# A hybrid decoder layer on one core: weight low parts on VectorE, table loads in the emission clock, TensorE ordered by the scheduler

## The chip, the cores and the metric

The kernel runs on one core of a Trainium2 chip. The metric is device time in microseconds, as the median of several executions; lower is better. One further execution was taken by the hardware profiler, and all rows below are of that one. The engines are TensorE (PE; its weight loads are listed as PEld), VectorE (DVE), ScalarE (ACT), GpSimd (POOL) and SyncE (SP), which issues DMAs.

## The reference

One layer over 512 prompt tokens and 32 sample tokens (8 sequences of 4), width 1024, all in float32:

```python
h = rmsnorm(x);  u = h @ w_in        # [HGRN2 q,f,i,g | RWKV-7 r,k,v, lora | gates]
o_a, s_a = hgrn2(u_a, s_a)           # 4 heads, 128x128 state, chunks of 64
o_b, s_b = rwkv7(u_b, s_b)           # 8 heads, 64x64 state, step by step:
#   S = S*w - (S@kk) (kk*a)^T + v k^T ;  y = S@r
x = x + (sigmoid(u_ga) * (o_a @ w_a_out) + sigmoid(u_gb) * (o_b @ w_b_out)) @ w_out
x = x + relu(rmsnorm(x) @ w_up)**2 @ w_down
y = rmsnorm(x)
```

The outputs are y, the new states of both branches and the last normalised row, each for prompt and samples.

## The kernel before

**Products.** All activations lie with channels on the partitions and the 544 tokens in the free dimension, in two halves of 272. Each float32 weight tile `st` (128x1024) is split by `split` into a high part `whi` (a copy on ACT to the matmul type fp32r) and a low part `wlo = st - whi`; a product is three passes, hi·hi, lo·hi and hi·lo. `w_in` is worked off in 46 column units of 128 columns; a unit is two `in_unit_ps` halves of 24 matmuls, 92 halves in all. The weight of a unit is loaded and split a few units ahead, in `ahead()`: there `wlo` is made on VectorE for the first units, and on GpSimd once more than `NDVE` = 11 units have been loaded.

**Lanes.** Between the matmuls of these halves the recurrences are worked off, in three lanes of generators: LX does the RWKV-7 heads in two groups of four (g0 from k0, k1, r0, r1, v0, v1; g1 from k2 to v3), LZ the low-rank parts (`lora_ps`) first, LY the four HGRN2 heads (`hg_head_*`), then the sample states (`rw_state`, `rw_sample`, `hg_sample`). The RWKV-7 steps of a group are, in order: `rw_batch_pa` for each of its head pairs (p0, p1 or p2, p3), the inverse of a triangular matrix on VectorE with DMAs through `zb_d` and `xz_d`, `rw_solve`, `rw_affine`, `rw_chain` and `rw_out`. The last writes `ob_d`, which the B branch reads back as `ob`.

**What sets the order.** While the kernel is built, a `Clock` keeps a planned time per engine. `Timed.cost` gives each instruction a planned duration. `gemm_h` calls `tick()` every 4 or 12 matmuls, and `tick` advances each lane whose planned readiness has come. So a lane's step is emitted after that many matmuls of the halves; the same clock chooses the next unit of the plan among `NEED` and `FILL`. From there the tile framework's scheduler orders the instructions of each engine by its own estimate of readiness. TensorE is taken out of that: the region of `manual_schedule(engines={PE})`, from the start of the lanes up to `drain(LY)` behind the B branch, leaves PE in the order of emission.

**Stages.** Norm and transposes (to 27 us), `w_in` with the lanes (to 541 us), the rest of g1 and of the samples, the B branch (16 groups `half_unit_ps` of 12 matmuls), the A branch (16 more), `w_out` (`pd`, from 655 us), `w_up`, `w_down` and the last norm. PSUM: `pse` is a single double bank, which `rw_batch_pa`, `lora_ps` and other steps of LX and LZ take in turn.

All instructions are issued by the helper `Timed.call`, so nearly all rows have its line (L160), and are told apart by the tile names.

Of the kernel before, what the change touches and what calls it, by code (L numbers as in the profile page):

```python
# [8 lines left out]
F32 = mybir.dt.float32  # L9
# [3 lines left out]
AF = mybir.ActivationFunctionType  # L13
ALU = mybir.AluOpType
# [30 lines left out]
PQ, LQ, ZQ, TQ = 0, 0, 1, 0  # L45
POOL_LO = 1
QUANT, FINE = 12, 4
NDVE = 11
NEED = "l0 k0 k1 r0 v0 r1 v1 l1 f0 q0 i0 g0 f1 q1 i1 g1 f2 q2 i2 g2 k2 k3 r2 r3 v2 v3 f3 q3 i3 g3"
FILL = "G8 G10 G2 G1 G3 G7 G13 G4 G11 G15 G9 G12 G5 G6 G14 G0"  # L50
X_WORK = "rw0 rw1"
# [4 lines left out]
class Clock:  # L56


    def __init__(self):
        self.ready, self.used, self.by, self.tags, self.busy = {}, {}, {}, {}, {}  # L60
        self.pe, self.gemm, self.lane, self.late = 0.0, True, None, []
# [4 lines left out]
    def place(self, eng, t, cost):  # L66
        b = self.busy.setdefault(eng, [])
        k = len(b)
        while k and b[k - 1][1] > t:
            k -= 1  # L70
        while k < len(b) and b[k][0] < t + cost:
            t = max(t, b[k][1])
            k += 1
        b.insert(k, (t, t + cost))
        while b and b[0][1] < self.pe - 60:
            b.pop(0)
        return t + cost
# [14 lines left out]
    def note(self, eng, cost, outs, ins, lane):  # L92
        for t in outs:
            self.first(t)
        r = 0.0
        for t, own in [(t, False) for t in ins] + [(t, True) for t in outs]:
            if self.by.get(t.name) != eng or (eng == "DMA" and not own):
                r = max(r, self.ready.get(t.name, 0.0))
            elif eng not in ("PE", "DMA"):
                r = max(r, self.ready[t.name] - 0.12)  # L100
            if own and not (eng in ("PE", "DMA") and self.by.get(t.name) == eng):
                r = max(r, self.used.get(t.name, 0.0))
        if eng == "PE":
            if r > self.pe + 0.2:
                self.late.append((self.pe, r - self.pe, outs[0].name))
            self.pe = end = max(self.pe, r) + cost
            end += 0.15
        elif eng == "DMA":
            end = r + cost
        else:  # L110
            end = self.place(eng, r, cost) + 0.12
        for t in ins:
            self.used[t.name] = max(self.used.get(t.name, 0.0), end)
        for t in outs:
            self.ready[t.name] = end
            self.by[t.name] = eng
            self.used[t.name] = max(self.used.get(t.name, 0.0), end)
        if lane is not None:
            lane.end = max(lane.end, end)


class Timed:


    def __init__(self, eng, name, clock):
        self.eng, self.name, self.clock = eng, name, clock

    def cost(self, fn, out, ops, kw):
        n = 1
        for d in out.shape[1:]:  # L130
            n *= d
        big = max([n] + [int(o.free_size()) for o in ops if hasattr(o, "tensor")])
        if self.name == "PE":
            gemm = len(ops) > 1 and ops[1].dtype == F32R
            switch = 0.12 if gemm != self.clock.gemm else 0.0
            self.clock.gemm = gemm
            if gemm:
                return n / 2400 + 0.013 + switch
            if fn == "transpose":
                return 0.11 * max(n, 32) / 128 + switch  # L140
            return max(n, 32) * (0.00085 if ops[0].shape[-1] >= 128 or n >= 128 else 0.0006) + switch
        if fn == "dma_start":
            return 2.3
        if self.name == "V":
            if fn == "reciprocal":
                return 0.1 + 0.0064 * n
            if fn == "tensor_tensor_scan":
                return 0.1 + 0.0022 * n
            return 0.15 + 0.00106 * big
        if self.name == "A":  # L150
            return 0.17 + 0.0009 * big
        if fn == "tensor_tensor":
            return 0.2 + 0.0025 * big
        return 0.3 + 0.0012 * big
# [25 lines left out]
def hybrid_step(ctx: ExitStack, tc: tile.TileContext, i, o):  # L180
    nc = tc.nc
    clock = Clock()
    V, A, P, T = (Timed(e, n, clock) for e, n in ((nc.vector, "V"), (nc.scalar, "A"), (nc.gpsimd, "P"), (nc.tensor, "PE")))
# [5 lines left out]
    def nm(s):  # L189
        uid[0] += 1  # L190
        return f"{s}{uid[0]}"
# [17 lines left out]
    def S(n, dt=F32, name="s"):  # L209
        return xp_.tile([128, 552], dt, tag="x", name=nm(name))[:, 0:n]  # L210
# [43 lines left out]
    def act(out, in_, func=AF.Copy, **kw):  # L254
        A.activation(out=out, in_=in_, func=func, **kw)

    def tt(out, a, b, op, eng=None):
        (eng or V).tensor_tensor(out=out, in0=a, in1=b, op=op)
# [27 lines left out]
    class W:  # L286
        pass

    def split(st, eng=None):
        w = W()  # L290
        w.hi = pipe.tile([128, 1024], F32R, tag="whi", name=nm("whi"))
        w.lo = pipe.tile([128, 1024], F32R, tag="wlo", name=nm("wlo"), bufs=3)
        act(w.hi, st)
        tt(w.lo, st, w.hi.bitcast(F32), ALU.subtract, eng)
        return w

    def load8(src, c):

        st = pipe.tile([128, 1024], F32, tag="stage", name=nm("st"), bufs=NST)
        SY.dma_start(out=st.rearrange("p (k c) -> p k c", k=8),  # L300
                          in_=src[:, c:c + 128].rearrange("(k p) c -> p k c", p=128))
        return st
# [78 lines left out]
    for u in STARTUP.split():  # L381
        if u == "w":
            pre = split(pre)
        elif u[0] == "s":
            stats(TORD[int(u[1])])
        else:
            {"t": transposed, "n": normed}[u[0]](TORD[int(u[1])], int(u[2]))
# [114 lines left out]
    def load4(src, c):  # L502

        st = pipe.tile([128, 1024], F32, tag="stage", name=nm("st"), bufs=NST)
        SY.dma_start(out=st.rearrange("p (k c) -> p k c", k=4),
                          in_=src[:, c:c + 256].rearrange("(k p) c -> p k c", p=128))
        return st
# [27 lines left out]
    def column(tok):  # L535
        n = int(tok[1:])
        if tok[0] in "lrkv":
            return B0 + 128 * ({"r": 0, "k": 4, "v": 8, "l": 12}[tok[0]] + n)
        return G0 + 128 * n if tok[0] == "G" else A0 + 512 * "qfig".index(tok[0]) + 128 * n

    need, fill, done, held, plan = NEED.split(), FILL.split(), set(), [0], []
    loaded, weights = {}, {column("l0"): pre}
# [13 lines left out]
    def ahead(c):  # L556

        for n, tok in enumerate(plan[0:3]):
            if tok not in loaded:
                loaded[tok] = load8(i["w_in"][0], column(tok))  # L560
        for tok in plan[0:2]:
            if tok in loaded and column(tok) not in weights:
                weights[column(tok)] = split(loaded[tok], P if len(loaded) > NDVE else V)
        return weights.pop(c)

    def in_unit(c, cuts=(0, HALF, TOK)):
        w = ahead(c)
        wh = [w.hi[:, 128 * k:128 * k + 128] for k in range(8)]
        wl = [w.lo[:, 128 * k:128 * k + 128] for k in range(8)]
        return gemm_h(wh, wl, [h_hi[:, k] for k in range(8)], [h_lo[:, k] for k in range(8)], cuts, "in_unit_ps")  # L570
# [26 lines left out]
    for kind in range(2):  # L597
# [3 lines left out]
        w = S(512, F32R, "lwd")  # L601
# [949 lines left out]
    def drain(*ls):  # L1551
        while any(L.work for L in ls):
            L = min((L for L in lanes if L.work and L.ready is not None), key=lambda L: L.ready)
            clock.pe = max(clock.pe, L.ready)
            if not advance(L):
                L.ready = min(M_.ready for M_ in lanes if M_.work and M_ is not L) + 0.01

    region = tc.manual_schedule(engines={mybir.EngineType.PE})
    region.__enter__()
    clock.start()  # L1560
    LZ.work.append(low_rank())
    for L, names in ((LX, X_WORK), (LY, Y_WORK)):
# [6 lines left out]
    while plan:  # L1569
        tok = plan.pop(0)  # L1570
# [55 lines left out]

    ob = branch(ob_d)
    wb = [split(load4(i["w_b_out"][0], 0))]
    for jp in range(4):
        if jp < 3:  # L1630
            wb.append(split(load4(i["w_b_out"][0], 256 * jp + 256)))
        w = wb[jp]
# [7 lines left out]
                r = slice(e * HALF, (e + 1) * HALF)  # L1640
                stt(mb[j][:, r], gt[:, r], 1.0, ps[e], ALU.add, ALU.mult)
    drain(LY)
    region.__exit__(None, None, None)
    pystack.close()
    psm = ctx.enter_context(tc.tile_pool(name="psm", bufs=2, space=bass.MemoryType.PSUM))

# [6 lines left out]
    for jp in range(4):  # L1653
        w = split(load4(i["w_a_out"][0], 256 * jp))
# [169 lines left out]
    for j in range(8):  # L1824
        st = load8(i["w_down"][0, 3072:4096], 128 * j)
        if j < 8 - NKEEP:
            w = []
# [7 lines left out]
        else:  # L1835
            w = split(st)
# [45 lines left out]
```

## Time and profile before

| | before |
| --- | --- |
| median of 3 runs (lowest to highest) | 1102.83 us (1100.08 to 1108.12) |
| profiled execution, device time | 1101.6 us |
| its span in the trace | 1099.9 us |
| PE busy over the span | 957.2 us (87%) |
| DVE, ACT, POOL busy | 577.3, 404.9, 198.5 us |
| share of the chain that ended last | PE 62%, DVE 15%, DMA 7%, ACT 7%, POOL 4% |

The profiled execution is 1.2 us below the median, and 1.7 us of it lie outside its span. Stages below are given in us from the span's start.

### The profile page before, as it was taken

The numbers are of one execution on the slowest core, as the hardware profiler recorded it, in microseconds if no ns is written. First come the engines' busy times: TensorE is split into PE (matmuls) and PEld (weight loads), VectorE is DVE, ScalarE is ACT, GpSimd is POOL, SyncE is SP. The second block draws the span as 40 slices with busy tenths as digits, with TensorE's granted clock in tenths as the row PEclk, the third lists the DMA queues.
The fourth block names the chain that finished last, engine by engine and source line by source line (L and its number), as shares of the span: only waits on it lengthen the run. The fifth ranks groups of instructions, "written<-read, shape, count | busy, mean of one in ns | idle before, by whom it ended". The sixth has DMA issues, their size and how long they took to land.

```text
span 1099.9 us, 21956 instructions
## 1 busy us (share of the span) xinstructions
PE 957.2 (87%) x9220; PEld 923.6 (84%) x9220; DVE 577.3 (52%) x1135; ACT 404.9 (37%) x761; POOL 198.5 (18%) x335
## 2 busy tenths in 40 slices
PE   5887778798987879779949599999999999999996
PEld 4787767787887878769738599999999999999996
DVE  6464639445766585713566585544432234444533
ACT  7451524546444433433231234334311123332332
POOL 4267443222254442221010000000000000000000
PEclk9798788899998889989968799999999999999998
DMA  8421323221133233341265445332333323233411
GB/s 241 135 85 53 101 69 74 74 60 42 60 100 101 78 93 69 92 121 43 79 185 183 156 127 157 88 97 78 96 87 87 95 78 97 79 104 90 133 39 44
DMA packets 191093, 106.40 MB, mean 97 GB/s; under 512 B 38946, under 2 KB 179048, under 8 KB 190995
## 3 DMA queue, kind: packets, MB, share of 16 engines
q1 hardware_dynamic: 165424, 95.16, 29.6%
q10 hardware_dynamic: 25570, 9.85, 3.5%
q8 instruction: 72, 1.18, 0.4%
q14 instruction: 27, 0.21, 0.1%
HBM read 85.08 MB, written 18.39 MB: 94 GB/s over the span
## 4 chain that ended last, share of the span: by engine, by line
PE 62%; DVE 15%; DMA 7%; ACT 7%; POOL 4%; issue 4%; SPq 1%; ACTq 1%; POOLq 0%; DVEq 0%
PE pd L160 21%; PE full_unit_ps L160 14%; PE in_unit_ps L160 14%; PE half_unit_ps L160 3%; DVE tmp L160 2%; DMA st<-in_w_down_dram 2%; ACT whi L160 1%; POOL lmk L394 1%; DVE wlo L160 1%; ACT L160 1%; DVE X L160 1%; DVE rs L160 1%; DVE bn L160 1%; PE lora_ps L160 1%; SPq L160 1%
## 5 line engine op out<-in xcount | busy, mean ns | idle before, releaser
L160 ACT ACTIVATE whi<-st 128x1024 fp32r<-128x1024 f32 x120 | 126.8, 1056 | 267.9 <-PE pd L160 117.7
L160 DVE TENSOR_TENSOR wlo<-st,whi 128x1024 fp32r<-128x1024 f32 x85 | 104.1, 1225 | 65.9 <-ACT whi L160 65.8
L160 PE MATMUL in_unit_ps<-h_hi,wlo 128*128 128x272 f32 (+3 forms) x736 | 122.2, 302 | 0.0
L160 PE MATMUL in_unit_ps<-h_hi,whi 128*128 128x272 f32 (+3 forms) x736 | 117.7, 304 | 3.5 <-ACT h_hi L160 3.3
L160 PE MATMUL in_unit_ps<-h_lo,whi 128*128 128x272 f32 (+3 forms) x736 | 111.6, 295 | 0.0
L160 PE MATMUL full_unit_ps<-hd,whi 128*128 128x272 f32 (+2 forms) x832 | 109.8, 288 | 0.0
L160 PEld LDWEIGHTS in_unit_ps<-h_hi,whi 128*128 128x128 f32 x736 | 104.8, 200 | 5.4 <-ACT h_hi L160 3.8
L160 PEld LDWEIGHTS in_unit_ps<-h_hi,wlo 128*128 128x128 f32 x736 | 105.3, 197 | 2.0 <-issue 0.3
L160 PEld LDWEIGHTS full_unit_ps<-hd,whi 128*128 128x128 f32 x832 | 106.2, 188 | 0.0
L160 POOL TENSOR_TENSOR wlo<-st,whi 128x1024 fp32r<-128x1024 f32 x35 | 85.8, 2451 | 98.6 <-ACT whi L160 97.4
L160 PEld LDWEIGHTS in_unit_ps<-h_lo,whi 128*128 128x128 f32 x736 | 102.3, 195 | 0.1
L160 POOL TENSOR_SCALAR ys<-ys,ssf 32x512 f32<-32x512 f32 x1 | 1.1, 1087 | 532.8 <-DVE ssf L160 532.8
L160 DVE SCALAR_TENSOR_TENSOR r<-pd,rsb 128x272 f32<-128x272 f32 x64 | 25.2, 436 | 90.5 <-PE pd L160 89.1
L160 PE MATMUL pd<-xgh,wlo 128*128 128x272 f32 x512 | 70.1, 288 | 0.0
L160 PE MATMUL pd<-xgh,whi 128*128 128x272 f32 x512 | 69.8, 288 | 0.0
L160 PE MATMUL pd<-xgl,whi 128*128 128x272 f32 x512 | 69.6, 287 | 0.0
L160 PEld LDWEIGHTS pd<-xgh,wlo 128*128 128x128 f32 x512 | 66.4, 188 | 0.0
L160 PEld LDWEIGHTS pd<-xgh,whi 128*128 128x128 f32 x512 | 66.3, 188 | 0.0
L160 PEld LDWEIGHTS pd<-xgl,whi 128*128 128x128 f32 x512 | 66.2, 188 | 0.0
L160 DVE TENSOR_TENSOR x<-x,full_unit_ps 128x272 f32<-128x272 f32 (+2 forms) x48 | 19.5, 435 | 71.6 <-PE full_unit_ps L160 71.6
L160 PE MATMUL full_unit_ps<-hd,wlo 128*128 128x272 f32 (+2 forms) x416 | 56.5, 288 | 0.0
L160 PEld LDWEIGHTS full_unit_ps<-hd,wlo 128*128 128x128 f32 x416 | 53.8, 188 | 0.0
(414 smaller groups left out, 1558.9 us busy)
## 6 DMA issues: line engine op xcount, KB each, us to landing
st<-in_w_in_dram SPq DMA_DIRECT2D x46, 512.0 KB
st<-in_w_up_dram SPq DMA_DIRECT2D x32, 512.0 KB
st<-in_w_down_dram SPq DMA_DIRECT2D x32, 512.0 KB
gt_d<-gt SPq DMA_DIRECT2D x16, 272.0 KB
st<-in_w_out_dram SPq DMA_DIRECT2D x8, 512.0 KB
gtb<-gt_d SPq DMA_DIRECT2D x8, 272.0 KB
gta<-gt_d SPq DMA_DIRECT2D x8, 272.0 KB
x<-xt_d SPq DMA_DIRECT2D x8, 272.0 KB
```

The source lines that it names most:

```text
L160: r = real(*a, **kw)
L394: return tc.keep_in_program_order(getattr(nc.gpsimd, name)(*a, **kw))
```

## The change

Three edits. `split` no longer takes an engine, so all low parts are made on VectorE; 35 of them were made on GpSimd. `Timed.cost` counts 1.3 us where an activation needs another function table than the last one, and 0.2 us for an accumulated output; this adds no instruction, but shifts the planned times, and with them the place of the lane steps among the matmuls and the choice of the next unit. And the manual region is gone, so the scheduler orders PE too.

```diff
-NDVE = 11
@@ class Timed
-        self.eng, self.name, self.clock = eng, name, clock
+        self.eng, self.name, self.clock, self.table = eng, name, clock, 0
@@ def cost
         if self.name == "A":
-            return 0.17 + 0.0009 * big
+            sets = {AF.Tanh: 1, AF.Exp: 1, AF.Sigmoid: 2, AF.Ln: 3, AF.Sqrt: 4}
+            new = sets.get(kw.get("func"), self.table)
+            load, self.table = 1.3 if new != self.table else 0.0, new
+            return 0.17 + 0.0009 * big + load + (0.2 if "accum_out" in kw else 0.0)
@@ def split
-        tt(w.lo, st, w.hi.bitcast(F32), ALU.subtract, eng)
+        tt(w.lo, st, w.hi.bitcast(F32), ALU.subtract)
@@ def ahead
-                weights[column(tok)] = split(loaded[tok], P if len(loaded) > NDVE else V)
+                weights[column(tok)] = split(loaded[tok])
@@ the lanes
-    region = tc.manual_schedule(engines={mybir.EngineType.PE})
-    region.__enter__()
     clock.start()
...
     drain(LY)
-    region.__exit__(None, None, None)
```

The order of the units in the plan is the same for the first 21; from there gates are drawn forward. k2, the first unit of g1, is the 25th before and the 28th after; v3, the last of g1, the 31st and the 35th. Seven units are left behind g3, the last one that a head needs, where nine were.

How PE's order moves is seen at two places. The first is about the eighteenth half, where the `lora_ps` steps of the gate stand. Before, on PE (a row is a run of matmuls, out<-moving,stationary, with its shape and count):

```order
L160 MATMUL in_unit_ps_1250<-h_lo,whi_980 128x272 x8
L160 MATMUL lora_ps_1276<-lx_391,lwh_375 128x272 x2
L160 MATMUL lora_ps_1276<-lx_391,lwl_376 128x272 x2
L160 MATMUL lora_ps_1276<-lx_392,lwh_375 128x272 x2
L160 MATMUL rw_batch_pa_1285<-kr_1009,eb_934 128x128 x8
L160 MATMUL lora_ps_1301<-lx_391,lwh_375 128x272 x2
```

And after, on PE at the same place:

```order
L162 MATMUL in_unit_ps_1248<-h_lo,whi_978 128x272 x8
L162 MATMUL in_unit_ps_1333<-h_hi,whi_1118 128x272 x8
L162 MATMUL in_unit_ps_1333<-h_hi,wlo_1119 128x272 x8
L162 MATMUL in_unit_ps_1333<-h_lo,whi_1118 128x272 x5
L162 MATMUL lora_ps_1274<-lx_391,lwh_375 128x272 x2
L162 MATMUL lora_ps_1274<-lx_391,lwl_376 128x272 x2
L162 MATMUL lora_ps_1274<-lx_392,lwh_375 128x272 x2
L162 MATMUL in_unit_ps_1333<-h_lo,whi_1118 128x272 x3
L162 MATMUL in_unit_ps_1387<-h_hi,whi_1118 128x272 x7
L162 MATMUL rw_batch_pa_1283<-kr_1007,eb_932 128x128 x8
```

The step stands 21 matmuls further back, and matmuls of the halves stand between it and `rw_batch_pa`. The second place is the solve of g1. Before, on PE:

```order
L160 MATMUL in_unit_ps_5555<-h_lo,whi_5300 128x272 x8
L160 MATMUL rw_solve_py_5604<-XT_5573,zb_4550 32x32 x16
L160 MATMUL rw_solve_py_5604<-XT_5573,zb_4790 32x32 x16
L160 MATMUL in_unit_ps_5672<-h_hi,whi_5413 128x272 x8
L160 MATMUL in_unit_ps_5672<-h_hi,wlo_5414 128x272 x4
L160 MATMUL rw_sample_ps_5685<-rs_5640 64x64 x8
L160 MATMUL rw_sample_pt_5695<-ident,bd_5653 128x128 x4
L160 MATMUL rw_solve_px_5702<-TT_5577,YT_5574 32x32 x16
```

And after, on PE, where `in_unit_ps_5767` is the 92nd and last half:

```order
L162 MATMUL in_unit_ps_5767<-h_lo,whi_5540 128x272 x6
L162 MATMUL rw_state_ps_5736<-ident,sn_5731 128x128 x4
L162 MATMUL in_unit_ps_5767<-h_lo,whi_5540 128x272 x2
L162 MATMUL rw_solve_py_5816<-XT_5785,zb_4637 32x32 x16
L162 MATMUL rw_solve_py_5816<-XT_5785,zb_4995 32x32 x16
L162 MATMUL rw_solve_px_5867<-TT_5789,YT_5786 32x32 x16
L162 MATMUL rw_solve_px_5867<-TT_5794,YT_5786 32x32 x16
L162 MATMUL rw_affine_pw_5944<-KA_5123,TT_5789 64x128 x6
```

Before, the solve of g1 stands behind the 84th half, and eight halves are spread over it and the steps behind it; after, all 92 halves are ahead of it. In the same way the last `rw_batch_pa` of g1 (pair p3) stands at half 73 before and 79 after. Most steps of `hg_sample`, which stand among the B branch before, are ahead of it after.

## Rows read from the trace of the kernel before

**Rows 1.** Windows: busy time of each engine (x instructions), granted PE clock, DMA.

```profile
27.00:655.00 628.00, 508.01 (x5680) 478.37 (x5680) 377.22 (x779) 245.94 (x475) 186.09 (x314) 0.89 0.32 93
655.00:1100.00 445.00, 434.65 (x3467) 433.21 (x3467) 182.22 (x292) 139.25 (x240) 1.09 (x1) 0.99 0.32 92
```

**Rows 2.** Windows, finer stretches of the first; columns PE, PEld, DVE, ACT, POOL.

```profile
27.00:419.00 392.00, 318.44 (x3414) 304.57 (x3415) 238.82 (x450) 170.81 (x317) 159.68 (x279) 0.90 0.28 79
419.00:488.00 69.00, 53.74 (x699) 51.42 (x700) 38.50 (x86) 25.86 (x66) 16.19 (x16) 0.93 0.41 100
...
541.00:566.00 25.00, 14.61 (x235) 10.28 (x232) 16.61 (x58) 8.76 (x21) 2.75 (x9) 0.71 0.51 129
...
575.00:623.00 48.00, 34.01 (x243) 31.36 (x243) 29.98 (x64) 7.48 (x12) 0.00 (x0) 0.78 0.51 161
```

**Rows 3.** Waits of PE, 27 to 655 us: total, times, longest.

```profile
PE hg_head_pt L160 <- DVE kh L160: 16.3, 4, 7.7
PE hg_head_pt L160 <- DVE hy L160: 16.1, 3, 8.2
PE lora_ps L160 <- DVE CB L160: 14.6, 2, 12.9
PE half_unit_ps L160 <- ACT oh L160: 11.3, 5, 6.4
PE head_sums_ps L160 <- POOL sxl L160: 6.9, 2, 6.2
```

**Rows 4.** Timeline of PE, 95 to 118 us: start, duration, what, idle before.

```profile
100.13 1.17 PE L160 MATMUL in_unit_ps<-h_hi,wlo 128*128 128x272 f32 x8
101.13 1.16 PE L160 MATMUL in_unit_ps<-h_lo,whi 128*128 128x272 f32 x8
115.24 0.79 PE L160 MATMUL lora_ps<-lx,lwh 128*128 128x272 f32 x2 [12.95 <-DVE CB L160]
```

**Rows 5.** Timeline of POOL, 80 to 118 us.

```profile
107.69 1.69 POOL L394 TENSOR_SCALAR_AFFINE_SELECT lmk<-lmk 32x32 f32<-32x32 f32 x6
109.46 0.40 POOL L160 TENSOR_TENSOR d<-U 128x24 f32<-128x24 f32 x2
```

**Rows 6.** Timeline of DVE, 95 to 118 us.

```profile
109.89 0.79 DVE L160 SCALAR_TENSOR_TENSOR xm<-d,prm,U 128x544 f32<-128x544 f32 x1 [13.72 <-POOL d L160]
```

**Rows 7.** Timeline of PE, pieces between 415 and 660 us.

```profile
417.69 1.16 PE L160 MATMUL rw_batch_pa<-kr,eb 64*128 64x128 f32 x16
...
487.85 1.20 PE L160 MATMUL rw_solve_py<-XT,zb 32*32 32x32 f32 x64
...
560.93 0.37 PE L160 MATMUL rw_out_pt<-ident,yo 64*64 64x64 f32 x2
...
574.68 1.14 PE L160 MATMUL half_unit_ps<-oh,whi 128*128 128x272 f32 x2 [3.64 <-ACT oh L160]
...
654.97 0.51 PE L160 MATMUL pd<-mh,whi 128*128 128x272 f32 x2 [0.30 <-ACT mh L160]
```

**Rows 8.** The page's groups: busy us, mean ns of one, idle before.

```profile
L160 DVE TENSOR_TENSOR wlo<-st,whi 128x1024 fp32r<-128x1024 f32 x85 | 104.1, 1225 | 65.9 <-ACT whi L160 65.8
...
L160 POOL TENSOR_TENSOR wlo<-st,whi 128x1024 fp32r<-128x1024 f32 x35 | 85.8, 2451 | 98.6 <-ACT whi L160 97.4
```

**Rows 9.** Timeline of DVE, 326 to 345 us.

```profile
328.21 2.84 DVE L160 SCALAR_TENSOR_TENSOR xm<-d,prm,U 128x544 f32<-128x544 f32 x1 [2.87 <-POOL d L160]
```

**Rows 10.** Timeline of POOL, 326 to 345 us.

```profile
328.13 2.34 POOL L160 TENSOR_TENSOR wlo<-st,whi 128x1024 fp32r<-128x1024 f32 x1
```

**Rows 11.** Timeline of ACT, 344 to 347 us.

```profile
344.75 1.28 ACT L160 ACT_TABLE_LOAD   x1
346.05 1.18 ACT L160 ACTIVATE nrm<-head_sums_ps 128x512 f32<-128x512 f32 x3
```

**Rows 12.** Timeline of DVE, 415 to 500 us.

```profile
419.90 0.42 DVE L160 TENSOR_TENSOR CB<-rw_batch_pa,msk 128x256 f32<-128x256 f32 x1
...
462.04 1.53 DVE L160 STREAM_TRANSPOSE XT<-D 32x256 f32<-32x256 f32 x4 [4.15 <-DMA D<-xz_d]
```

More of the change, by code (lines that the diff above doesn't have):

```diff
@@ L287, in hybrid_step, with split @@
         pass
-    def split(st, eng=None):
+    def split(st):
         w = W()
```

## The prediction

> **What bounds the kernel now.** I read the windows first. Behind 655 us PE is busy for 434.7 of 445 us at a granted clock of 0.99; nothing is to be had there, and the change doesn't touch that part. From 27 to 655 us PE is busy for 508.0 of 628 us at 0.89, so some 120 us are idle; DVE is busy for 377.2, ACT for 245.9, POOL for 186.1 [rows 1]. No engine is full in this stretch: PE waits for the chains of the recurrences. The finer windows say where. 27 to 419 us holds 73.6 us of idle PE at a clock of 0.90, 419 to 488 another 15.3, 541 to 566 another 10.4 with the clock at 0.71, 575 to 623 another 14.0 with 0.78 [rows 2]. The waits name the ends: HGRN2 steps that wait for DVE (16.3 and 16.1 us), `lora_ps` for DVE's `CB` (14.6, of it 12.9 at once), `head_sums` for POOL (6.9), the branches for `oh` (11.3) [rows 3]. At the longest the reader sees what kind of wait it is: `in_unit_ps` matmuls run until 102 us, then PE stands 12.95 us before a `lora_ps` [rows 4], although the next halves of the GEMM depend on nothing in that chain. POOL was making masks until 109.4 us and only then a small `d`, for which DVE had waited 13.72 us [rows 5, 6]; behind it DVE came to the `CB` that frees the PSUM bank. So these are waits of program order: the step was emitted by a planned time that came too early, and the GEMM behind it was blocked.
>
> **PE ordered by the scheduler.** The `lora_ps` step now stands 21 matmuls further back, and the GEMM runs ahead of it; most steps of the lanes move back by one to six halves in the same way. PE still works in the order written, and that order is a guess on readiness: a step put too early stalls as before. The trace has no run of the new order, so the return lies between nothing and the 73.6 us idle before 419 us [rows 2]. The first two kinds of waits, for `kh` and `hy`, are at the end of long DVE chains that a scheduler sees; the wait behind POOL's masks is one of small instructions whose number, not size, matters. I take 33 us, a bit under half, since the longest wait is of the second kind.
>
> Now the sum, by events on PE. Before, the last `rw_batch_pa` of g1 starts at 417.69 us [rows 7]. In the new order it stands behind 79 halves, not 73. Eight matmuls take 1.00 us from start to start [rows 4], so a half is 3.0 and six are 18 us. With 33 us of idle gone: 417.7 + 18 − 33 = 403.
>
> From there to the solve of g1 it took 70.2 us before [rows 7], with 53.7 busy of 69 [rows 2] and 11 halves in it. Now 13 halves stand there: 6 us more, 59.7 busy; of the 15.3 idle I keep half: 67 us, so 470. The inverse hides in it: from `CB` at 419.90 to the end of the transposes at 463.57 is 43.7 us [rows 12], and 24 us passed before between that end and the solve. That is slack of program order which the new order fills with GEMM.
>
> From the solve to `rw_out` it took 73.1 us [rows 7], with eight halves, 24 us, in it. Now all 92 halves are ahead, so the bounds are 49 us, if every half had lain on the path, and 73, if the chain of DVE, ACT and PE steps sets the time by itself. Steps of `hg_sample` move into this stretch from the B branch, and DVE was busy there for 16.6 of 25 us between 541 and 566 us [rows 2], so I take 60: 530.
>
> From `rw_out` to the first `half_unit_ps` are 13.8 us of DMA out, DMA in and split [rows 7]; unchanged: 544. From there to `w_out` it took 80.3 us [rows 7]. The 32 groups of 12 matmuls at 0.125 us are 48 us; the rest is idle or at the lower clock, 14.0 us of it waits in 575 to 623 [rows 2]. With much of `hg_sample` out of the way the bounds are 48 and 80; I take 68, nearer to the old value because A's operands come last there and PE waited 6.4 us for them [rows 3]: 612. What follows took 1101.6 − 655.0 = 446.6 us [rows 7], unchanged. The sum is 1058.6 against the profiled 1101.6, and with the 1.2 us by which the median stands above it, **1060 us**.
>
> **Low parts on VectorE.** 35 `wlo` leave POOL, 85.8 us, and cost DVE 35 × 1.225 = 42.9 us [rows 8]. What comes back is that DVE is no longer held up by them: one `xm` took 2.84 us while a POOL `wlo` of 2.34 us began 0.08 us ahead of it, where the same operation took 0.79 at another place [rows 6, 9, 10]. So between nothing and 35 × 2.05 = 72 us of DVE time return. In both cases DVE stays under two thirds busy [rows 1], and the weight of a unit is due a few units, some 6 us each, ahead. POOL, busy for 186 of 628 us, is freed. I price it at nothing for PE; the ends are −5 us (a `head_sums` that waits for `sxl` behind a `wlo`, 6.9 us in all [rows 3]) and +5 (a DVE step of a chain behind four 1.2 us subtractions), and they lie within the choices above.
>
> The Trainium skill ("VectorE: DVE Perf Modes", on the second SBUF read interface shared with GpSimd) bears that out for `xm`, which has two SBUF inputs. It would make the return the larger one, and the sum a few us lower.
>
> **Table loads in the clock.** Nothing is added to ACT by itself. A load takes 1.28 us and the next activation starts 1.30 us behind its start [rows 11], so the planned 1.3 is the measured one. Its effect is the later place of the steps and the plan in which g1's units come three to four units later; both are counted above, as the 18 us. If the scheduler had ordered the steps well anyway, this part is a loss of that size.
>
> The Trainium skill ("ScalarE: Activation LUTs", What ACT_TABLE_LOAD costs) puts a switch at 1.28 us and 1.38 of drain, 2.66 in all. The trace disagrees: the activation follows at once [rows 11]. By the page the planned time would be 1.36 us too short per load, steps would stand too early, and more of the 33 us would stay as waits.
>
> **Rivals.** First, slower. The GEMM is the only filler that PE has, and the new order spends all 92 halves before the solve. If the waits ahead of it stay (none of the 73.6 us goes), the last `rw_batch_pa` comes at 436, the solve 75 us later at 511, the chain, naked now and with `hg_sample` on DVE in front of it, takes the old 73: 584, B at 598. With the clock low for its first part as between 541 and 566 us (0.71 [rows 2]) B and A take 80 to 85, and the end is 1125 to 1130. It decides at about 420 us: if `rw_batch_pa` of p3 isn't earlier than that, the halves that went ahead of it are a loss. For it speaks that the new positions are later throughout; against it, that 24 us of known slack go in any case.
>
> The Trainium skill ("TensorE: Matmul & The Clock Gate", HAM oscillation) warns that idle gaps between bursts of matmuls drop the clock to its lower level, which speaks against a chain without filler; the 0.71 and 0.78 of [rows 2] agree with it.
>
> Second, no change. The lanes, not PE, set the stage: the chains of DVE and ACT have their own length, waits only move from one step to the next, and the solve comes when it did, at about 488. Then only the halves behind it shorten the rest: 488 + 66 + 14 + 78 + 447 + 1 = 1094 to 1103. For it speaks that DVE is busy for 60% and its steps depend on each other; against it that PE's waits before 419 us are few and long, and at those the GEMM is ready.
>
> Third, better than forecast: nine tenths of the idle time before 419 us go (66 us), the chain takes 49 and the branches 60: `rw_batch_pa` at 370, solve 430, `rw_out` 479, B 493, `w_out` 553, the end 1001 us. It needs a scheduler that guesses every chain right.
>
> **How the numbers follow.** A measurement of this kernel tells about 1% from no change. Forecast, with its own 1016 to 1091: 0.68; third rival, 0.06; no change, 0.13; slower, 0.13. Faster by over 1% is 0.74, within 1% 0.13, slower 0.13. The range of 1016 to 1106 leaves out most of the slower and of the third case, under 2 in 10.
>
> **What would show it.** The 12.95 us before `lora_ps` and the 6 us before `head_sums` gone or moved to another step; idle PE before the last `rw_batch_pa` of 40 us, not 74; that step at about 403; the solve at 470 behind the last half; a stretch of about 75 us from the solve to B with PE half idle and the clock near 0.7; `w_out` at about 612 and the same 447 us behind it. `xm` at 0.8 us everywhere. The forecast is wrong if waits before 419 us stay above 65 us in new places, or if solve to `w_out` takes over 165 us.

## The result

The changed kernel takes 1054.76 us (1051.74 to 1056.61, 4 runs) against 1102.98 (1100.08 to 1108.12): a ratio of 0.9555 with a 95% interval of 0.9512 to 0.9599. The forecast was 1060. The profiled execution took 1051.7 us with a span of 1050.0.

First the windows of the changed kernel, cut at its own events (the last `rw_batch_pa` of g1, its solve, its `rw_out`, the B branch, the A branch, `w_out`); the columns are those of [rows 1].

```profile
27.00:388.00 361.00, 326.68 (x3544) 313.43 (x3543) 240.94 (x478) 177.38 (x327) 105.08 (x252) 0.95 0.32 92
388.00:451.00 63.00, 58.51 (x739) 57.08 (x738) 41.40 (x91) 25.71 (x63) 4.71 (x10) 0.95 0.44 114
451.00:516.00 65.00, 49.36 (x799) 38.96 (x799) 31.66 (x95) 18.82 (x44) 3.04 (x8) 0.79 0.15 35
516.00:537.50 21.50, 10.61 (x133) 7.45 (x131) 14.39 (x44) 6.19 (x16) 2.34 (x9) 0.52 0.64 182
537.50:575.00 37.50, 34.13 (x245) 30.05 (x243) 27.25 (x59) 8.28 (x13) 0.00 (x0) 0.86 0.65 211
575.00:604.00 29.00, 28.69 (x218) 28.69 (x219) 24.52 (x50) 10.70 (x15) 0.00 (x0) 0.94 0.43 139
604.00:1050.00 446.00, 436.37 (x3481) 434.92 (x3480) 183.34 (x294) 139.90 (x241) 1.09 (x1) 0.99 0.32 92
```

Up to the last `rw_batch_pa` 34.3 us of PE are idle where 73.6 were [rows 2], and the clock is granted at 0.95, not 0.90. Of the idle time behind it most lies between 451 and 537.5 us, where 26.5 of 86.5 us are idle and the clock falls to 0.79 and then 0.52, little above the lower of its two levels (1.2 of 2.4 GHz, which is 0.50). Behind 604 us nothing has changed [rows 1].

The events, in the timeline of PE (they answer to [rows 7]):

```profile
387.99 1.16 PE L162 MATMUL rw_batch_pa<-kr,eb 64*128 64x128 f32 x16
...
451.21 0.98 PE L162 MATMUL rw_solve_py<-XT,zb 32*32 32x32 f32 x50
...
515.81 1.18 PE L162 MATMUL rw_out_pt<-ident,yo 64*64 64x64 f32 x32 [2.37 <-DVE yo L162]
...
528.05 1.97 PE L162 MATMUL rw_out_pt<-ident,yo 64*64 64x64 f32 x32 [0.96 <-DVE yo L162]
...
537.45 0.89 PE L162 MATMUL half_unit_ps<-oh,whi 128*128 128x272 f32 x3
...
600.08 1.66 PE L162 MATMUL pd<-mh,whi 128*128 128x272 f32 x12
```

The last `rw_batch_pa` comes 29.7 us earlier than before, although six halves more stand ahead of it; the solve 36.6, `rw_out` 45.1, B 37.2 earlier.

PE's waits in the changed kernel, 27 to 610 us, against [rows 3]:

```profile
PE head_sums_ps L162 <- POOL sxl L162: 20.1, 4, 13.4
...
PE half_unit_ps L162 <- ACT oh L162: 2.8, 3, 1.7
...
PE hg_head_pt L162 <- DVE kh L162: 2.0, 1, 2.0
PE lora_ps L162 <- DVE CB L162: 1.9, 1, 1.9
...
PE hg_head_pt L162 <- DVE hy L162: 1.1, 1, 1.1
```

32.4 us of waits for `kh` and `hy` have become 3.1; 14.6 for `CB` have become 1.9. One wait has grown by much: `head_sums` for GpSimd's `sxl`, 6.9 to 20.1. It is the old wait behind the masks at another step, as PE and POOL show at 101 us:

```profile
101.86 0.82 PE L162 MATMUL head_sums_ps<-sxl,bones 128*128 128x272 f32 x2 [13.41 <-POOL sxl L162]
```

```profile
99.36 0.57 POOL L396 TENSOR_SCALAR_AFFINE_SELECT lmk<-lmk 32x32 f32<-32x32 f32 x2
...
100.48 1.33 POOL L162 TENSOR_TENSOR sxl<-rk,sxh 128x544 fp32r<-128x544 f32 x1
```

### The profile page after: what moved, and what is told of

It is laid out like the page before. It is cut to its first block, busy times and chain, and to the rows that moved or that the text cites. A ratio compares the mean times of both kernels' runs of the same rounds, so it can differ in the third digit from the quotient of the medians.

```text
span 1050.0 us, 21959 instructions
## 1 busy us (share of the span) xinstructions
PE 959.4 (91%) x9220; PEld 923.6 (88%) x9220; DVE 580.4 (55%) x1170; ACT 406.1 (39%) x763; POOL 127.7 (12%) x300
## 4 chain that ended last, share of the span: by engine, by line
PE 65%; DVE 10%; DMA 3%; ACT 3%; issue 2%; POOL 1%; ACTq 1%; SPq 0%; DVEq 0%; POOLq 0%
PE pd L162 23%; PE full_unit_ps L162 18%; PE in_unit_ps L162 11%; PE half_unit_ps L162 4%; DVE tmp L162 1%; DVE rs L162 1%; PE rw_affine_pw L162 1%; PE rw_affine_pq L162 1%; DVE wlo L162 1%; PE rw_chain_pc L162 1%; DVE E L162 1%; DVE X L162 1%; DVE bn L162 1%; PE hg_sample_po L162 1%; DVE gs L162 1%
## 5 line engine op out<-in xcount | busy, mean ns | idle before, releaser
L162 DVE TENSOR_TENSOR wlo<-st,whi 128x1024 fp32r<-128x1024 f32 x120 | 147.1, 1225 | 82.3 <-ACT whi L162 82.0
L162 PE MATMUL in_unit_ps<-h_hi,wlo 128*128 128x272 f32 (+3 forms) x736 | 118.5, 297 | 0.0
L162 PEld LDWEIGHTS in_unit_ps<-h_hi,wlo 128*128 128x128 f32 x736 | 102.8, 193 | 1.3 <-issue 0.3
L162 ACT ACTIVATE gt<-in_unit_ps 128x272 f32<-128x272 f32 x32 | 12.6, 394 | 47.5 <-PE in_unit_ps L162 35.7
```

The source lines that it names most:

```text
L162: r = real(*a, **kw)
```

## The experiments

Three theories stood at the start. A, that of the prediction: the order of TensorE carries the gain and the low parts on VectorE are worth nothing. B: what counts is where a step is emitted. Compared after the prediction, the orders show that this place is set by the engine on which the clock plans the low parts and hardly by the table loads: with table loads alone the last `rw_batch_pa` of g1 stands at half 74 (73 before), with the low parts alone at 79. C: VectorE is relieved, since GpSimd's low parts hold up its instructions.

**Each edit alone.** `e_order` takes only the region out, `e_wlo` has only the low parts on VectorE, `e_table` only the table loads.

```diff
# e_order: the kernel before, with
-    region = tc.manual_schedule(engines={mybir.EngineType.PE})
-    region.__enter__()
...
-    region.__exit__(None, None, None)
# e_wlo: the kernel before, with
-                weights[column(tok)] = split(loaded[tok], P if len(loaded) > NDVE else V)
+                weights[column(tok)] = split(loaded[tok])
# e_table: the kernel before, with the lines of class Timed from the change
```

> The kernel before with only the manual region removed: the scheduler orders TensorE, low parts still on GpSimd, no table loads in the clock. Places in its order: lora_ps steps late as in the changed kernel (from half 8), but rw_batch_pa of p3 at half 73 and the solve of g1 at half 84, as before. Theory A (the order of TensorE carries the gain): 1060 to 1075 us. Theory B (what counts is that steps are emitted later, which the clock sets from the engine of the low parts): 1085 to 1100, since only the early steps move. Theory C (VectorE freed from GpSimd's low parts): 1095 to 1105.

> The kernel before with only the low parts on VectorE: TensorE in program order, no table loads in the clock. The clock now plans these subtractions on VectorE, so the program order itself shifts: rw_batch_pa of p3 at half 79, not 73, the solve of g1 behind half 92, not 84. Theory A: within 1095 to 1110 (later steps cost 18 us, fewer waits give it back). Theory B: 1065 to 1080, most of the gain. Theory C: 1075 to 1090.

> The kernel before with only the table loads counted in the emission clock. In its program order rw_batch_pa of p3 stands at half 74 (73 before), the solve of g1 behind half 85 (84): the prediction put the later places down to this edit, and the order shows that they come with the low parts. If that is so, no change: 1098 to 1110. If planned loads still keep steps from being emitted too early: 1080 to 1095.

Measured: `e_order` 1082.01 us, ratio 0.9797 (0.9748 to 0.9846); `e_wlo` 1077.55, 0.9768 (0.9719 to 0.9818); `e_table` 1093.58, 0.9909 (0.9875 to 0.9943). `e_order` lies in none of its three ranges: the order alone is worth 23 us, not 43, and not nothing either. So A fails as it stood, since the low parts alone are worth as much (27 us, in the ranges of both B and C). `e_table` lies in the range of its second case: it was expected to bring nothing and brings 10 us, with the last `rw_batch_pa` and the solve hardly later in the order. In `e_order` PE's waits for VectorE stay, although the scheduler orders PE:

```profile
PE head_sums_ps L160 <- POOL sxl L160: 25.0, 5, 13.4
PE hg_head_pt L160 <- DVE kh L160: 17.1, 4, 7.5
PE hg_head_pt L160 <- DVE hy L160: 10.6, 3, 6.1
```

The scheduler expects `kh` and `hy` where VectorE doesn't deliver them: 27.7 us of waits, of 32.4 before [rows 3]. The 12.9 us for `CB` go and come back as a wait for `sxl`. So the last `rw_batch_pa` of g1 starts only 5.4 us earlier, at 412.3; the solve follows at 471.5, 11 us closer to it than before [rows 7], which is the slack of program order, and the branches give the rest (69.5 us from B to `w_out`, 74.3 before).

**Engine or place.** `w_engine` and `w_clock` split `e_wlo`: the first moves the work to VectorE and plans it as GpSimd's, the second leaves it on GpSimd and plans it as VectorE's.

```diff
     SY = Timed(nc.sync, "S", clock)
# w_engine
+    X = Timed(nc.vector, "P", clock)
# w_clock
+    X = Timed(nc.gpsimd, "V", clock)
# both
-                weights[column(tok)] = split(loaded[tok], P if len(loaded) > NDVE else V)
+                weights[column(tok)] = split(loaded[tok], X if len(loaded) > NDVE else V)
```

> The kernel before with the 35 low parts on VectorE, but planned in the emission clock as if on GpSimd: the program order of TensorE is the one before, only the engine differs. Theory A and B: 1095 to 1105, no change. Theory C: all of what the low parts on VectorE give, 1075 to 1090.

> The kernel before with the 35 low parts on GpSimd as before, but planned in the emission clock as if on VectorE: the program order of TensorE is that of the low parts on VectorE (p3 at half 79, solve of g1 behind half 92), the engines are those before. Theory A: 1100 to 1115. Theory B: 1065 to 1085. Theory C: 1100 to 1110.

Measured: `w_engine` 1080.58 us, 0.9783 (0.9726 to 0.9841); `w_clock` 1098.20, 0.9957 (0.9932 to 0.9982). The engine is worth 24 us with every step in its old place; the place alone some 5. That is C, against A and B (`w_clock` lies 2 us below C's range). `e_wlo` and `w_clock` are such a pair as well: in both traces PE's instructions come in the same order, and the low parts on VectorE instead of GpSimd are worth 20.7 us there (1077.55 and 1098.20). The page's first part of `w_engine` and its group of low parts show the relief:

```profile
PE 960.5 (89%) x9220; PEld 928.2 (86%) x9220; DVE 577.4 (53%) x1170; ACT 405.7 (38%) x761; POOL 123.2 (11%) x300
...
L160 DVE TENSOR_TENSOR wlo<-st,whi 128x1024 fp32r<-128x1024 f32 x120 | 146.8, 1224 | 84.9 <-ACT whi L160 84.9
```

VectorE does 35 low parts more, 42.7 us against [rows 8], and is busy for 577.4 us where it was for 577.3. So everything else on it takes 42.6 us less (430.6 for 473.2). Its `xm`, 1377 ns on average before, shows it, and with it go 15 us of PE's waits for `kh` and `hy` (17.4 for 32.4). First `xm`, then these waits, both of `w_engine`:

```profile
L160 DVE SCALAR_TENSOR_TENSOR xm<-d,prm,U 128x544 f32<-128x544 f32 x14 | 11.3, 807 | 16.9 <-POOL d L160 16.8
```

```profile
PE hg_head_pt L160 <- DVE hy L160: 9.6, 3, 5.8
...
PE hg_head_pt L160 <- DVE kh L160: 7.8, 3, 3.2
```

`w_clock` tells what a later place does: the last `rw_batch_pa` of g1 comes at 416.5 us with six halves more ahead of it (417.7 before [rows 7]), so PE has lost some 19 us less in waits and at the lower clock; `rw_out` comes 8.8 us later, since no half is left beside the chain, and `w_out` 7.0 us earlier, since more of the samples is done by then. The waits for `kh` and `hy` all but go there too, although nothing is relieved: 5.0 us are left, and 5.6 in `e_wlo` (27 to 600 us; `w_clock`, then `e_wlo`):

```profile
PE hg_head_pt L160 <- DVE kh L160: 5.0, 2, 4.2
```

```profile
PE hg_head_pt L160 <- DVE kh L160: 4.1, 1, 4.1
...
PE hg_head_pt L160 <- DVE hy L160: 1.5, 1, 1.5
```

So these two waits don't measure what the relief is worth. Between `w_clock` and `e_wlo` they are as long, and yet the last `rw_batch_pa` comes 18.1 us earlier (at 398.4 us), with some 14 us less of idle PE ahead of it, spread over several other waits.

**What on GpSimd costs.** Is it that its operations hold up VectorE's, or that its queue is full? `d_two` and `d_one` put idle work on GpSimd at the places of the low parts in `w_engine`.

```diff
# w_engine, with
+    junk = const.tile([128, 128], F32, name="junk")
...
+                if len(loaded) > NDVE:
# d_two
+                    for _ in range(5):
+                        late.tensor_tensor(out=junk, in0=junk, in1=junk, op=ALU.subtract)
# d_one
+                    for _ in range(7):
+                        late.tensor_scalar(out=junk, in0=junk, scalar1=1.0, scalar2=0.0, op0=ALU.mult, op1=ALU.add)
```

> w_engine (low parts on VectorE, program order of before), with five GpSimd subtractions of 128x128 on a tile of its own at the place of each low part that left: two SBUF inputs, about 2.4 us together, waiting for nothing, their result used by nobody. Theory C1 (a two-input GpSimd operation holds up VectorE instructions beside it): the gain goes, 1095 to 1115, and xm takes over 2 us beside them. C2 (GpSimd's queue is kept busy, so its small copies and sxl come late): 1090 to 1105, with xm at 0.8. C3 (in the kernel before, GpSimd's queue stood waiting for ACT's whi): 1078 to 1086.

> As d_two, with seven GpSimd tensor_scalar operations of 128x128 with one SBUF input in place of the five subtractions, of about the same time together. C1 with two inputs as its condition: 1078 to 1088, and xm at 0.8. C1 with any GpSimd operation: as d_two. C2: 1090 to 1105. C3: 1078 to 1086.

Measured: 1096.47 us, 0.9926 (0.9897 to 0.9955), and 1096.13, 0.9932 (0.9909 to 0.9956). Both lose about 16 of the 24 us. In their groups one sees how long GpSimd was taken, and that `xm` was hardly held up (`d_two`, then `d_one`):

```profile
L160 DVE SCALAR_TENSOR_TENSOR xm<-d,prm,U 128x544 f32<-128x544 f32 x14 | 11.9, 849 | 18.4 <-POOL d L160 18.2
L397 POOL TENSOR_TENSOR junk<-junk 128x128 f32<-128x128 f32 x175 | 101.5, 580 | 11.5
```

```profile
L160 DVE SCALAR_TENSOR_TENSOR xm<-d,prm,U 128x544 f32<-128x544 f32 x14 | 11.4, 811 | 18.7 <-POOL d L160 18.5
L397 POOL TENSOR_SCALAR junk<-junk 128x128 f32<-128x128 f32 x245 | 107.6, 439 | 17.8
```

With hardly any hold-up PE's waits for `kh` and `hy` are back at what they were, 32.2 us in `d_two` and 31.5 in `d_one` (`d_two`):

```profile
PE hg_head_pt L160 <- DVE kh L160: 17.5, 3, 7.4
PE hg_head_pt L160 <- DVE hy L160: 14.7, 3, 9.2
```

So C2: a taken queue costs by itself, since GpSimd's small copies (`el`, `xi`, `pw`) come late; VectorE's waits for these three rise from 3.4 us in `w_engine` to 11.6 in `d_two` and 13.8 in `d_one`. It doesn't follow that the queue was the loss in the kernel before. There the two waits of this kind (`el` and `xi`) were 3.5 us in all, as in `w_engine`; in `w_clock` and `e_wlo` they are 9.2 us each. So they don't depend on where the low parts are made, while the hold-up does: 42.6 us, and 39.2 by the same sum in `w_clock` against `e_wlo`. The idle work held up VectorE by 10.8 us (two inputs) and 4.9 (one), taken as its busy time without low parts, 441.4 and 435.5 against 430.6. The idle work was also longer than the low parts, 101.5 and 107.6 against 85.8 us, and waited for nothing. C3, that GpSimd's queue stood waiting for `whi` in the kernel before, had foreseen no loss from idle work, and there was one. What such waiting costs was not tested; only the unchanged waits for `el` and `xi` speak against it. How the 24 us divide between hold-up and queue stays open.

The Trainium skill ("VectorE: DVE Perf Modes", Two Vector instructions with no wait between them) has a VectorE instruction with two SBUF inputs read one of them through an interface that it shares with GpSimd; `xm` is such an instruction, and its 1377 to 807 ns agree.

**Two edits together.** `e_order_wlo` is the changed kernel without the table loads.

```diff
# the kernel before, with the edits of e_order and of e_wlo
```

> The changed kernel without the table loads in the clock: TensorE ordered by the scheduler and the low parts on VectorE. If the two single edits add up (0.980 and 0.977 of the kernel before) and the table loads do nothing: 1053 to 1062. If the table loads carry part of the gain: 1065 to 1075. If both single edits remove the same waits: 1070 to 1078, and then the table loads must bring the rest.

Measured: 1052.44 us, 0.953 (0.9469 to 0.9592). Order and low parts add up (0.9797 × 0.9768 = 0.957), and no gain of the table loads is seen beside them (0.9555 for all three, within the interval): the 10 us that they bring alone don't come on top.

**The wait that is left.** `m_masks` builds the masks later.

```diff
-        if count in (3, 7, 10):
-            (consts1, consts2, consts3)[(3, 7, 10).index(count)]()
+        if count in (3, 9, 14):
+            (consts1, consts2, consts3)[(3, 9, 14).index(count)]()
```

> The changed kernel with GpSimd's mask building emitted later: the second and third group at the 9th and 14th unit in place of the 7th and 10th, so that sxl of the second head pair stands ahead of the masks on GpSimd. In the changed kernel TensorE waits 13.4 and 4.9 us for sxl there. If TensorE's idle time ahead of g1 is what sets the time: 12 to 18 us less, 1036 to 1043. If the lanes (VectorE, ACT) set the time and the wait only hides theirs: 1050 to 1058.

Measured: 1040.26 us, 0.9407 (0.9367 to 0.9447), some 15 us less than the changed kernel (10.2 between the two profiled executions) and the lowest median of all. The wait for `sxl` falls from 20.1 to 4.5 us, 10.1 of it come back as one wait of `head_sums` for ACT:

```profile
PE head_sums_ps L162 <- ACT sxh L162: 10.6, 2, 10.1
...
PE head_sums_ps L162 <- POOL sxl L162: 4.5, 4, 2.2
```

The last `rw_batch_pa` is 10.1 us earlier, by 6.7 us less of idle PE and 3.3 us of shorter work at a granted clock of 0.96, and `w_out` 11.5 earlier: what is won far ahead of the chain is passed on to `w_out` in full.

**The filler that is spent.** In the changed kernel the transposes for g1's solve end at 432.3 us, ACT's part at 434.8, and the solve starts at 451.2 behind the last half. `f_hold3` keeps three gate units back until the solve is emitted; `f_hm3` does so with the later masks; `s_swap` is `f_hm3` with `hg_sample` ahead of the RWKV-7 sample states.

```diff
# f_hold3: the changed kernel, with
+        while len(plan) + len(need) + len(fill) == 3 and 1 not in solved:
+            ... advance the lane that is ready first, as drain() does
         tok = plan.pop(0)
...
         yield from rw_solve(pairs)
+        solved.append(g)
# f_hm3: f_hold3 and the edit of m_masks
# s_swap: f_hm3, and
-Y_WORK = "hg0 hg1 hg2 hg3 rs hs"
+Y_WORK = "hg0 hg1 hg2 hg3 hs rs"
```

> The changed kernel with the last three gate units (six halves) emitted only after the solve of g1: in its order the solve stands behind half 87, not 92, and the rest lies beside rw_affine and rw_chain. In the changed kernel the operands of the solve are ready at 434.8 us and the solve starts at 451.2, and then the chain runs without filler with the clock at 0.79. If that spending of filler costs: solve at 435 to 440, solve to rw_out a little over the 65 us of before, 1038 to 1046. If halves beside the chain delay each of its steps as much as they fill: 1050 to 1058. If the clock, kept up by them, shortens the chain: below 1038.

> Both edits, later masks and three gate units held back. If they are independent: the sum of the two, 1020 to 1032. If the lanes set the time, no more than the better of the two.

> Both edits of f_hm3, and in lane LY hg_sample ahead of the RWKV-7 sample states (rw_state, rw_sample). With three gate units held back the chain of g1 came 11 us earlier and the A branch did not: it waited 6.4 us for the last step of hg_sample, which ended at 566 us as in the changed kernel. If that lane was the second bound, with hg_sample early the 11 us come through: 1026 to 1034. If the sample work is only exchanged, and the B branch now waits for the RWKV-7 samples: 1040 to 1055.

Measured: `f_hold3` 1052.46 us, 0.9518 (0.9472 to 0.9564), no different from the changed kernel; `f_hm3` 1042.62, 0.9432 (0.9392 to 0.9472), no different from `m_masks`; `s_swap` 1043.09, 0.9428 (0.94 to 0.9455), the same. `f_hold3` lies in the range for halves that delay the chain, but that is not what happened. The solve did come early, most of it at 434 to 436 us; B began at 526.8, 10.6 us earlier; and then the A branch didn't follow (0.9 us earlier than in the changed kernel), as PE's timeline shows:

```profile
526.81 1.47 PE L162 MATMUL half_unit_ps<-oh,whi 128*128 128x272 f32 x4 [1.64 <-ACT oh L162]
...
572.54 1.83 PE L162 MATMUL half_unit_ps<-oh,whi 128*128 128x272 f32 x6 [6.42 <-ACT oh L162]
```

Its operands need the last step of `hg_sample` on VectorE, which came when it did in the changed kernel; VectorE in `f_hold3`, and then in the changed kernel:

```profile
566.27 0.72 DVE L162 SCALAR_TENSOR_TENSOR hs<-hg_sample_pt,prm,ga 128x32 f32<-128x32 f32 x4
```

```profile
565.90 0.72 DVE L162 SCALAR_TENSOR_TENSOR hs<-hg_sample_pt,prm,ga 128x32 f32<-128x32 f32 x4
```

So lane LY with its samples is a second bound that ends within a few us of g1's chain. `s_swap` confirms it from the other side: with `hg_sample` early the longest wait of PE at the start of the A branch is 0.4 us, and B begins at 533.2, not 517.6 as in `f_hm3`, behind PE's waits for `rw_sample`:

```profile
PE rw_sample_pt L162 <- DVE rs L162: 6.2, 1, 6.2
...
PE rw_sample_ps L162 <- DVE rs L162: 3.7, 1, 3.7
```

`w_out` starts at 589.4 in `f_hm3` and 589.1 in `s_swap`. The work is exchanged, as the second expectation had it.

## Why the prediction was right, step by step

**What bounds.** Right in the main: more than half of PE's idle time ahead of 419 us went (39.3 of 73.6 us), and the tail stayed. Of the signs that were named, `xm` at 0.8 us came (785 ns on average), and the 12.95 us moved to another step, where they are 13.41.

**Up to the last `rw_batch_pa`.** 403 us was forecast, 388.0 came. Of the 73.6 us idle 39.3 went (33 foreseen). The rest is for the most part the clock, which the sum had left out: PE is busy for 326.7 us there, where 316.4 before 417 us and 18 for six halves make 334.4. With fewer gaps the granted clock is 0.95, and about the same matmuls take 7.7 us less.

**To the solve.** 67 us forecast, 63.2 measured; the solve stands right behind the last half, as foreseen.

**Solve to `rw_out`, and to B.** 60 and 13.8 forecast, 64.6 and 21.6 measured. The chain without filler is longer than I took it, at a clock of 0.79, and B waits for the second pair of `rw_out`, 12.2 us behind the first with steps of `hg_sample` between. That these steps come into this place was foreseen; that they delay B was not counted.

**B to `w_out`, and the tail.** 68 and 446.6 forecast, 62.6 and 451.7 measured. Here the cut was wrong: 654.97 us is a wait in the midst of `w_out`. Its first `pd` stood at 648.99 us before, in PE's timeline:

```profile
648.99 1.66 PE L160 MATMUL pd<-mh,whi 128*128 128x272 f32 x12
```

So the branches took 74.3 us and the tail 452.6. The two errors cancel in the sum; against the right figure the branches shortened by 11.7 us, 12.3 being forecast.

**The low parts at nothing** is the step that failed: 5 us either way were allowed for, and alone they are worth 24. The sum of VectorE was in the text, 42.9 us of added work against up to 72 returned, and 42.6 returned; but from VectorE's load I took it that this time costs PE nothing (the load is 60%; "under two thirds in both cases" is just missed at 66.9% if nothing returns). Part of it lay in the chains to `kh` and `hy`. I let the scheduler remove the waits for them, and by itself it didn't: 27.7 us of 32.4 stay in `e_order`. The relief about halves them (17.4 in `w_engine`), the later place takes most of them even without relief (5.0 in `w_clock`), and in the changed kernel 3.1 are left. That the total held is luck: the prediction put under the order a gain about as large as order and low parts bring together.

**The later places** were put down to the table loads and priced at a loss of 18 us. They come with the low parts, through the planned clock, and are no loss: in `w_clock` the later step comes at the old time with 18 us more of GEMM behind it.

**The rivals.** The slower one was to be decided at 420 us, and `rw_batch_pa` came at 388. Its mechanism is there, the chain without filler at a low clock, but `f_hold3` shows that filler would not help: lane LY ends at the same time. No change is excluded by the interval.

## What to carry to other kernels

An engine at 60% load can still set the time, if its instructions stand in the chains for which the bound engine waits: price a relief by what waits for the chain, not by the load. Where a planner's clock decides the order, an edit of an engine moves the order as well; a run with the engine changed and the plan kept, and one the other way, tells the two apart. And a chain that is shortened alone gives nothing if a second lane ends a few us behind it.

## What was not expected of the hardware

35 subtractions of 85.8 us on GpSimd made the rest of VectorE's work 42.6 us longer, about half of their own time. GpSimd operations on 128x128, five to seven in a row, of more time together, made it only 4.9 to 10.8 us longer, and still took back some 16 of the 24 us; VectorE's waits for GpSimd's small copies rose by 8.2 to 10.4 us beside them.
